# One plain gate/up pair fewer in every FFN, ScalarE's and VectorE's order in gate/up fixed, and the fourth product ahead of the third

## The chip, the cores and the metric

The kernel runs on one core of a Trainium2 chip. The metric is the device time of one execution in microseconds; the time before is the median of three runs. A change of less than about 0.2% is not told from none.

## What is computed

Two layers of a decoder trunk on 512 tokens of width 1024, in float32. Each layer has an FFN with half weight, a mixer (a gated linear recurrence beside a windowed attention) and a second FFN with half weight, each between two RMS norms. The change touches the gate/up part of the four FFNs:

```python
def swiglu(h, w_gate, w_up, w_down):
    return (jax.nn.silu(h @ w_gate) * (h @ w_up)) @ w_down

for l in range(DEPTH):                       # DEPTH = 2, D_MODEL = 1024, D_FF = 2816
    h = rms_norm(x, gn[0])
    x = x + 0.5 * rms_norm(swiglu(h, w_ffn1_gate[l], w_ffn1_up[l], w_ffn1_down[l]), gn[1])
    ...                                      # the mixer
    h = rms_norm(x, gn[4])
    x = x + 0.5 * rms_norm(swiglu(h, w_ffn2_gate[l], w_ffn2_up[l], w_ffn2_down[l]), gn[5])
```

## The kernel before

**Numbers in two halves.** Each float32 operand is split into a high half (`hi`, rounded to float32r by a cast on ScalarE) and a low half (`lo`, what the rounding left). A product is three matmuls, hi by hi, hi by lo, lo by hi (`mm3`); the low half of the weights is used by the third. The low half is made in one of two ways: VectorE subtracts `hi` from the source (L332 for weights, L402 for values), or ScalarE writes the negated source, rounded as `hi` is, into `lo` (L329) and GpSimd issues a DMA that adds the source to it (L330).

**Gate/up.** D_FF = 2816 gives 22 column tiles of 128, each a gate tile and an up tile, called a pair here. The first two pairs are computed together in `quad`. Then come plain pairs: for gate and for up eight matmul triples of 512 columns (`project`), and `gated` multiplies Silu(gate) by up. After `PLAIN` pairs (`FIRST` in the very first FFN) the rest of the 22 is done in `fast`: each pair is a 2 x 2 block product with seven products instead of eight (`sevenths`), each product being four matmul triples of 256 columns. A seven-product pair needs, beside the raw values, sums over quarters of x: `pre.sums()` makes them in four rounds, each some additions on VectorE (L459 to L466, L564) and two splits (casts L401, subtractions L402). In the first FFN a round also scales x (L535) and splits it.

**Weights.** `Stream` brings weights from HBM in order: a raw ring `w32` of W32 = 4 tiles loaded by SyncE, and rings `whi` and `wlo` of WS = 6 tiles. A plain pair uses two raw tiles as they are (kind `u`, VectorE subtracts; kind `v`, low half by DMA). A seven-product pair makes four pieces of its two raw tiles, in this order: **a**, the first tile (low half by DMA; products 1 and 2), **b**, two additions on VectorE (L312, L313; products 5 and 7), **c**, two more additions on b (L318, L319; products 6 and 4), **d**, half of the second tile (low half by DMA; product 3). `ahead` splits up to `most` = AHEAD = 3 items past the current one while fewer than WS are in flight; what it splits stands in the program at that place.

**After the products.** In `sevenths` ScalarE copies product 1 (L865), VectorE combines (L875, L877, L882, L883) into `m`, which has one buffer; ScalarE takes Silu on half of it (L895) and VectorE multiplies into z (L896).

**What sets the order.** TensorE's order is that of the program. The other engines' instructions are ordered by a scheduler when the kernel is built, except that those given to `pin` keep the program's order among themselves. In before only some are pinned: the additions of b and c, and the gating multiplication.

The seven products in before, in order: 1 and 2 (piece a), 5 and 7 (b), 6 (c), 3 (d), 4 (c again).

Of the kernel before, what the change touches and what calls it, by code (L numbers as in the profile page):

```python
# [7 lines left out]
F32 = mybir.dt.float32  # L8
F32R = mybir.dt.float32r
I32 = mybir.dt.int32  # L10
AF = mybir.ActivationFunctionType
# [34 lines left out]
def trunk(ctx: ExitStack, tc: tile.TileContext, xin, wall, gains, lbT, hgain, sinks, c_dist, c_mask, c_ident, out):  # L46
# [12 lines left out]
    def nm(s):  # L59
        seq[0] += 1  # L60
        return f"{s}_{seq[0]}"
# [94 lines left out]
    class Stream:  # L156
        def __init__(self):
            self.n, self.wall = 0, 0
            self.items = []
            self.raw, self.dma = {}, 0  # L160
            self.done, self.flight = 0, 0
            self.cur, self.c = 0, 0
            self.src = {}
            self.pinned = False
            self.most = AHEAD
            self.side, self.freed = {}, 0

        def plain(self, n, kind="u"):
# [86 lines left out]
        def quarter(self, it):  # L255
# [34 lines left out]
            if it.kind in ("p5", "p4"):  # L290
                self.raw.pop(it.u)
                self.freed += 1
                self.load(self.freed + W32)

        def split(self):
            it = self.items[self.done]
            if it.kind[0] == "p":
                return self.quarter(it)
            u, last = it.u, it.kind in "uvd"
            self.load(u + (1 if it.kind in "uv" else 2))  # L300
            it.hi = sb.tile([P, D], F32R, tag="whi", name=nm("whi"), bufs=WS)
            it.lo = sb.tile([P, D], F32R, tag="wlo", name=nm("wlo"), bufs=WS)
            w, h = self.raw[u], (slice(0, D // 2), slice(D // 2, D))
            cols = (slice(0, D),)
            if it.kind == "u" and u == 0:
                cols = h
            if it.kind in "bcd":
                v = self.raw[u + 1]
            if it.kind == "b":

                self.t13 = sb.tile([P, D], F32, tag="tt", name=nm("tt"), bufs=2)
                pin(nc.vector.tensor_tensor(self.t13[:, h[0]], w[:, h[0]], v[:, h[0]], op=ALU.add))  # L312
                pin(nc.vector.tensor_tensor(self.t13[:, h[1]], v[:, h[0]], v[:, h[1]], op=ALU.add))  # L313
                w = self.t13
            elif it.kind == "c":

                t = sb.tile([P, D], F32, tag="tt", name=nm("tt"), bufs=2)
                pin(nc.vector.tensor_tensor(t[:, h[0]], self.t13[:, h[0]], v[:, h[1]], op=ALU.add))  # L318
                pin(nc.vector.tensor_tensor(t[:, h[1]], t[:, h[0]], w[:, h[1]], op=ALU.add))  # L319
                w = t  # L320
            elif it.kind == "d":
                w = v
                cols = h[1:]
            for c in cols:
                i = nc.scalar.copy(it.hi[:, c], w[:, c])  # L325
                if u < 3 or self.pinned:
                    pin(i)
                if it.kind in "vad":
                    nc.scalar.mul(it.lo[:, c], w[:, c], -1.0)  # L329
                    nc.gpsimd.dma_start(it.lo[:, c].bitcast(F32), w[:, c], accum_op=ALU.add)  # L330
                else:
                    nc.vector.tensor_tensor(it.lo[:, c], w[:, c], it.hi[:, c].bitcast(F32), op=ALU.subtract)  # L332
# [64 lines left out]
    def split(src, scale=None, to=None):  # L397

        hi, lo = to or (big(F32R), big(F32R))
        if scale is None:  # L400
            nc.scalar.copy(hi, src)  # L401
            nc.vector.tensor_tensor(lo, src, hi.bitcast(F32), op=ALU.subtract)  # L402
# [448 lines left out]
    def sevenths(pre, between=lambda: None):  # L851

        def product(o, it, c, n):
            x = pre.operand(n)
            for k in range(4):
                wmm(o, ws.block(it, c + k), x[k], k == 0, k == 3)

        p1, p26, p57, p43 = acc()[:, :H2], acc(), acc(), aux()  # L860
        s, v = big()[:, :H2], big(F32, [P, 2, H2])
        m = sb.tile([P, 4, H2], F32, tag="m", name=nm("m"), bufs=1)
        w = ws.whole()
        product(p1, w, 0, 1)
        nc.scalar.copy(s, p1)  # L865
# [9 lines left out]
        nc.vector.tensor_tensor(m[:, 0:4:2, :], pairs[0], s.unsqueeze(1).to_broadcast([P, 2, H2]), op=ALU.add)  # L875

        nc.vector.tensor_tensor(v, pairs[1], m[:, 2:3, :].to_broadcast([P, 2, H2]), op=ALU.add)  # L877
        w = ws.whole()
        product(p43[:, H2:], w, 4, 3)
        product(p43[:, :H2], c, 4, 4)  # L880

        nc.vector.tensor_tensor(m[:, 3, :], p57[:, :H2], v[:, 1, :], op=ALU.add)  # L882
        nc.vector.tensor_tensor(m[:, 1:3, :], pairs[2], v[:, ::-1, :], op=ALU.add)  # L883
        return m

    def fast(pre, a, start):
        def early():
            if j == FT - 1:
                for i in range(EARLY):
                    a[i] = split(a[i])  # L890

        for j in range(start, FT):
            m = sevenths(pre, early)
            z = big(F32, [P, 2, H2])
            nc.scalar.activation(out=m[:, 0:2, :], in_=m[:, 0:2, :], func=AF.Silu)  # L895
            nc.vector.scalar_tensor_tensor(z, m[:, 0:2, :], -1.0, m[:, 2:4, :], op0=ALU.mult, op1=ALU.mult)  # L896
            a.append(z.rearrange("p i t -> p (i t)"))

    def ffn(l, n, pre, nxt, halves=True):
        a = []  # L900
# [24 lines left out]
        if first:  # L925
            gated(o[4], o[5])
            for j in range(3, FIRST):
                if j > 3:
                    order.until(lambda: pre.laid)
                    pre.sums()  # L930
                if j == 4:
                    pre.sums()
                gated(project(pre), project(pre))
            fast(pre, a, FIRST)
        else:
            for j in range(2, PLAIN):
                pre.sums()
                gated(project(pre), project(pre))
            fast(pre, a, PLAIN)
# [512 lines left out]
```

## Time and profile before

| | |
|---|---|
| median of three runs | 2100.99 us (2100.95 to 2102.06) |
| profiled execution | 2100.66 us |
| its span, first to last instruction | 2098.9 us |
| granted TensorE clock, mean | 0.999 |
| busy: PE, PEld, DVE, ACT, POOL | 100%, 89%, 74%, 53%, 7% |

Names in the profile: PE is the matmul stream of TensorE and PEld its weight load, DVE is VectorE, ACT ScalarE, POOL GpSimd, SP SyncE. L115 is the line in `mm` that issues matmuls, so matmuls are told apart by the tiles they write: a plain pair writes `acc` tiles with 512 columns, a seven-product pair three `acc` tiles and one `aux` tile with 256 columns. In a timeline row the first number is the start in microseconds from the span's start, the second the duration; brackets give idle time of the engine before it and what ended it. A DMA row ends with the size in KB and the time from issue to landing in microseconds.

### The profile page before, as it was taken

The page shows a single profiled execution, that of the slowest core. Times are in us where ns is not written, and L with a number is a line of the kernel's source. Part 1 is how long each engine was busy: PE and PEld are TensorE (multiplying, and loading weights), DVE is VectorE, ACT ScalarE, POOL GpSimd, SP SyncE. Part 2 cuts the span into 40 slices and gives each one's busy share as a digit, 9 for nine tenths or more (in the row PEclk, how much of TensorE's full clock was granted, in tenths as well). Part 3 has the DMA queues.
Part 4 walks back from the last instruction along what each step waited for, and adds up shares of the span by engine and source line. Part 5 has one row for each costly group of instructions (what it writes and reads, how often), then busy time and mean ns, then how long its engine had stood idle before and what let it go on. Part 6 is the DMA issues. An engine that isn't in the chain of part 4 may idle for free.

```text
span 2098.9 us, 35207 instructions
## 1 busy us (share of the span) xinstructions
PE 2090.3 (100%) x13549; PEld 1875.3 (89%) x13549; DVE 1550.5 (74%) x2705; ACT 1122.4 (53%) x1899; POOL 154.2 (7%) x188
## 2 busy tenths in 40 slices
PE   9999999999999999999999999999999999999998
PEld 8899988887888999998899998898778989999987
DVE  5877886766776777789587778767687758777884
ACT  6555564456454555556455556554653545555562
POOL 0011000000000011110001110000000000111000
PEclk9999999999999999999999999999999999999999
DMA  8577653312236357774447775632122563677651
GB/s 246 152 181 184 178 157 135 111 61 71 71 101 203 127 122 182 181 198 122 154 114 176 183 181 150 191 120 92 51 81 61 136 193 103 159 182 181 184 160 51
DMA packets 148071, 298.35 MB, mean 142 GB/s; under 512 B 16992, under 2 KB 74816, under 8 KB 147904
## 3 DMA queue, kind: packets, MB, share of 16 engines
q1 hardware_dynamic: 122416, 228.16, 33.2%
q0 software_dynamic: 25344, 67.91, 18.7%
q8 instruction: 106, 1.74, 0.3%
q14 instruction: 61, 0.50, 0.1%
q10 hardware_dynamic: 144, 0.05, 0.0%
HBM read 213.43 MB, written 14.73 MB: 109 GB/s over the span
## 4 chain that ended last, share of the span: by engine, by line
PE 88%; DMA 0%; DVE 0%; ACT 0%; SPq 0%; issue 0%; ACTq 0%
PE acc L115 64%; PE aux L115 22%; PE aux L125 1%; PE acc L125 1%; DMA wlo<-w 0%; DMA w<-wall 0%; SPq L241 0%; DVE s L402 0%; ACT whi L282 0%; DVE s L731 0%; ACT s L600 0%; DVE s L712 0%; DVE s L896 0%; DVE wlo L287 0%; ACT m L895 0%
## 5 line engine op out<-in xcount | busy, mean ns | idle before, releaser
L115 PE MATMUL acc<-s,whi 128*128 128x256 f32 (+1 forms) x4952 | 1059.3, 311 | 0.4 <-ACT whi L325 0.3
L115 PEld LDWEIGHTS acc<-s,whi 128*128 128x128 f32 x4952 | 808.0, 191 | 51.3 <-issue 3.2
L115 PE MATMUL acc<-s,wlo 128*128 128x256 f32 (+1 forms) x2476 | 766.6, 310 | 0.1
L115 PEld LDWEIGHTS acc<-s,wlo 128*128 128x128 f32 x2476 | 472.6, 191 | 25.0 <-DVE wlo L332 0.4
L325 ACT CAST whi<-w 128x1024 fp32r<-128x1024 f32 (+1 forms) x341 | 316.6, 948 | 237.6 <-PE acc L115 95.5
L115 PE MATMUL acc<-whi,s 128*128 128x512 f32 x1264 | 413.6, 393 | 0.1
L325 ACT CAST whi<-tt 128x1024 fp32r<-128x1024 f32 x154 | 161.4, 1048 | 326.5 <-DVE tt L319 184.2
L332 DVE TENSOR_TENSOR wlo<-w,whi 128x1024 fp32r<-128x1024 f32 (+1 forms) x181 | 218.3, 1215 | 151.4 <-ACT whi L325 149.6
L115 PEld LDWEIGHTS acc<-whi,s 128*128 128x128 f32 x1264 | 237.1, 188 | 54.7 <-ACT whi L325 1.6
L332 DVE TENSOR_TENSOR wlo<-tt,whi 128x1024 fp32r<-128x1024 f32 x154 | 188.1, 1221 | 98.8 <-ACT whi L325 98.7
L115 PE MATMUL acc<-wlo,s 128*128 128x512 f32 x632 | 246.4, 390 | 0.0
L115 PE MATMUL aux<-s,whi 128*128 128x256 f32 (+1 forms) x1248 | 230.4, 285 | 0.0
L330 POOL DMA_DIRECT2D wlo<-w x160 | 137.8, 863 | 1258.6 <-ACT wlo L329 704.9
L115 PE MATMUL aux<-whi,s 128*128 128x512 f32 x592 | 196.7, 390 | 0.0
L115 PEld LDWEIGHTS aux<-s,whi 128*128 128x128 f32 x1248 | 195.2, 192 | 1.1 <-issue 0.5
L115 PE MATMUL aux<-s,wlo 128*128 128x256 f32 (+1 forms) x624 | 177.5, 284 | 0.0
L115 PEld LDWEIGHTS acc<-wlo,s 128*128 128x128 f32 x632 | 118.7, 188 | 23.4
L115 PEld LDWEIGHTS aux<-whi,s 128*128 128x128 f32 x592 | 111.1, 188 | 22.8
L329 ACT ACTIVATE wlo<-w 128x1024 fp32r<-128x1024 f32 (+1 forms) x160 | 129.8, 844 | 0.0
L401 ACT CAST s<-s 128x512 fp32r<-128x512 f32 (+1 forms) x164 | 88.4, 580 | 71.5 <-DVE s L460 67.9
L115 PEld LDWEIGHTS aux<-s,wlo 128*128 128x128 f32 x624 | 119.8, 192 | 0.3
L115 PE MATMUL aux<-wlo,s 128*128 128x512 f32 x296 | 115.2, 389 | 0.0
(186 smaller groups left out, 2128.6 us busy)
## 6 DMA issues: line engine op xcount, KB each, us to landing
w<-wall SPq DMA_DIRECT2D x267, 512.0 KB, 3.7
wlo<-w POOLq DMA_DIRECT2D x83, 512.0 KB, 5.5
w<-wall SPq DMA_DIRECT2D x288, 128.0 KB, 3.3
wlo<-w POOLq DMA_DIRECT2D x77, 256.0 KB, 3.3
x_d<-s SPq DMA_DIRECT2D x48, 256.0 KB, 2.1
s<-x_d SPq DMA_DIRECT2D x48, 256.0 KB, 5.5
w<-wall SPq DMA_DIRECT2D x34, 256.0 KB, 3.0
s<-wall SPq DMA_DIRECT2D x64, 128.0 KB, 3.6
```

What stands on the lines that cost most here:

```text
L115: nc.tensor.matmul(o, lhsT, rhs, start=start, stop=stop)
L125: nc.tensor.transpose(o, src, ident)
L325: i = nc.scalar.copy(it.hi[:, c], w[:, c])
L329: nc.scalar.mul(it.lo[:, c], w[:, c], -1.0)
L330: nc.gpsimd.dma_start(it.lo[:, c].bitcast(F32), w[:, c], accum_op=ALU.add)
L332: nc.vector.tensor_tensor(it.lo[:, c], w[:, c], it.hi[:, c].bitcast(F32), op=ALU.subtract)
L401: nc.scalar.copy(hi, src)
```

## The change

It does five things. `PLAIN` goes from 4 to 3 and `FIRST` from 7 to 6, so each FFN has one plain pair fewer and one seven-product pair more; the four rounds of sums are issued within the pairs that are left. Inside `fast` (`ws.tight`) the casts, the multiplications by -1, the subtractions, the copy of product 1, the combinations, Silu and z are pinned to the program's order. The multiplication into z is held back (`ws.gate`) and issued behind the additions of the next b that is split, or before the next `m` is taken. Product 4 comes ahead of product 3, so that piece c is done before d is needed. And `most` is AHEAD + 1 in all but the last seven-product pair. The order of products 4 and 3 also changes in the mixer's `branches`, which use `sevenths` without the pinning.

```diff
-W32, WS, AHEAD, TAIL, PLAIN, FIRST, EARLY, LATE = 4, 6, 3, 4, 4, 7, 4, 8
+W32, WS, AHEAD, TAIL, PLAIN, FIRST, EARLY, LATE = 4, 6, 3, 4, 3, 6, 4, 8
...
+        def hold(self, i):
+            if self.tight:
+                pin(i)
+
+        def product(self):
+            if self.gate:
+                self.gate()
+                self.gate = None
...  (in Stream.split, kind b, behind the two additions)
+                self.product()
...
                 i = nc.scalar.copy(it.hi[:, c], w[:, c])
-                if u < 3 or self.pinned:
+                if u < 3 or self.pinned or self.tight:
                     pin(i)
                 if it.kind in "vad":
-                    nc.scalar.mul(it.lo[:, c], w[:, c], -1.0)
+                    self.hold(nc.scalar.mul(it.lo[:, c], w[:, c], -1.0))
                     nc.gpsimd.dma_start(it.lo[:, c].bitcast(F32), w[:, c], accum_op=ALU.add)
                 else:
-                    nc.vector.tensor_tensor(it.lo[:, c], w[:, c], it.hi[:, c].bitcast(F32), op=ALU.subtract)
+                    self.hold(nc.vector.tensor_tensor(it.lo[:, c], w[:, c], it.hi[:, c].bitcast(F32), op=ALU.subtract))
...  (in sevenths)
-        m = sb.tile([P, 4, H2], F32, tag="m", name=nm("m"), bufs=1)
...
-        nc.scalar.copy(s, p1)
+        ws.hold(nc.scalar.copy(s, p1))
...
         product(p26[:, H2:], c, 0, 6)
+        ws.product()
+        m = sb.tile([P, 4, H2], F32, tag="m", name=nm("m"), bufs=1)
...  (the four combinations are held likewise)
-        w = ws.whole()
-        product(p43[:, H2:], w, 4, 3)
         product(p43[:, :H2], c, 4, 4)
+        product(p43[:, H2:], ws.whole(), 4, 3)
...  (in fast)
+        ws.tight = True
         for j in range(start, FT):
+            ws.most = AHEAD + (j < FT - 1)
             m = sevenths(pre, early)
             z = big(F32, [P, 2, H2])
-            nc.scalar.activation(out=m[:, 0:2, :], in_=m[:, 0:2, :], func=AF.Silu)
-            nc.vector.scalar_tensor_tensor(z, m[:, 0:2, :], -1.0, m[:, 2:4, :], op0=ALU.mult, op1=ALU.mult)
+            ws.hold(nc.scalar.activation(out=m[:, 0:2, :], in_=m[:, 0:2, :], func=AF.Silu))
+
+            def gate(m=m, z=z):
+                ws.hold(nc.vector.scalar_tensor_tensor(z, m[:, 0:2, :], -1.0, m[:, 2:4, :], op0=ALU.mult, op1=ALU.mult))
+
+            ws.gate = gate
+            if j == FT - 1:
+                ws.product()
             a.append(z.rearrange("p i t -> p (i t)"))
+        ws.tight = False
...  (in ffn, first FFN)
                 if j > 3:
                     order.until(lambda: pre.laid)
                     pre.sums()
-                if j == 4:
                     pre.sums()
...  (other FFNs)
             for j in range(2, PLAIN):
+                pre.sums()
                 pre.sums()
```

Three places show what moved in the built programs. The numbers in the rows of before and after are different names for the same kind of tile; after's lines stand 11 to 20 further down.

First, VectorE in the first FFN, where piece b of the first seven-product pair stands (L312, L313, L332 in before). Before, behind the third round of sums (its last two subtractions, L402):

```order
L402 TENSOR_TENSOR s_734<-s_727,s_733 128x512
L402 TENSOR_TENSOR s_738<-s_728,s_737 128x512
L312 TENSOR_TENSOR tt_798<-w_92_503,w_104_567 128x512
L313 TENSOR_TENSOR tt_798<-w_104_567 128x512
L332 TENSOR_TENSOR wlo_797<-tt_798,whi_796 128x1024
L905 TENSOR_TENSOR s_803<-acc_741,s_395 128x512
L907 TENSOR_TENSOR s_804<-acc_771,s_395 128x512
```

After, behind the second round, ahead of the gating (L925, L927) of the plain pair that in before stood ahead of the third round:

```order
L413 TENSOR_TENSOR s_639<-s_632,s_638 128x512
L413 TENSOR_TENSOR s_643<-s_633,s_642 128x512
L322 TENSOR_TENSOR tt_703<-w_72_384,w_78_437 128x512
L323 TENSOR_TENSOR tt_703<-w_78_437 128x512
L343 TENSOR_TENSOR wlo_702<-tt_703,whi_701 128x1024
L925 TENSOR_TENSOR s_708<-acc_646,s_395 128x512
L927 TENSOR_TENSOR s_709<-acc_676,s_395 128x512
```

Piece b moved ahead of one gating step and of the third round. Between the third and the fourth round in after stands nothing, where before had piece b and one gating step; piece c follows the fourth round in both.

Second, ScalarE at the same entry: the casts of pieces c (`whi<-tt`), d and the next pair's a, with the multiplications for the low halves, and the Silu of the last plain pair. Before:

```order
L325 CAST whi_859<-tt_861 128x1024
L325 CAST whi_891<-w_104_567 128x512
L329 ACTIVATE wlo_892<-w_104_567 128x512
L325 CAST whi_916<-w_133_676 128x1024
L906 ACTIVATE s_900<-s_900 128x512
L329 ACTIVATE wlo_917<-w_133_676 128x1024
```

After:

```order
L336 CAST whi_789<-tt_791 128x1024
L336 CAST whi_821<-w_78_437 128x512
L340 ACTIVATE wlo_822<-w_78_437 128x512
L926 ACTIVATE s_830<-s_830 128x512
L336 CAST whi_842<-w_92_503 128x1024
L340 ACTIVATE wlo_843<-w_92_503 128x1024
```

The Silu, which waits for VectorE's gating step, moved ahead of the cast of the next pair's piece a.

Third, VectorE in a pair in the middle of gate/up, from the combinations to the next pair's. Before:

```order
L875 TENSOR_TENSOR m_8299<-acc_8294,s_8297 128x2x256
L877 TENSOR_TENSOR s_8298<-acc_8295,m_8299 128x512
L332 TENSOR_TENSOR wlo_8365<-tt_8366,whi_8364 128x1024
L882 TENSOR_TENSOR m_8299<-acc_8295,s_8298 128x256
L883 TENSOR_TENSOR m_8299<-aux_8296,s_8298 128x512
L896 SCALAR_TENSOR_TENSOR s_8417<-m_8299 128x512
L312 TENSOR_TENSOR tt_8462<-w_1484_8263,w_1485_8265 128x512
L313 TENSOR_TENSOR tt_8462<-w_1485_8265 128x512
L332 TENSOR_TENSOR wlo_8461<-tt_8462,whi_8460 128x1024
```

After:

```order
L887 TENSOR_TENSOR m_8379<-acc_8289,s_8292 128x2x256
L889 TENSOR_TENSOR s_8293<-acc_8290,m_8379 128x512
L893 TENSOR_TENSOR m_8379<-acc_8290,s_8293 128x256
L894 TENSOR_TENSOR m_8379<-aux_8291,s_8293 128x512
L322 TENSOR_TENSOR tt_8426<-w_1483_8239,w_1484_8241 128x512
L323 TENSOR_TENSOR tt_8426<-w_1484_8241 128x512
L911 SCALAR_TENSOR_TENSOR s_8413<-m_8379 128x512
L343 TENSOR_TENSOR wlo_8425<-tt_8426,whi_8424 128x1024
```

The multiplication into z (L896, now L911) moved behind the additions of b, and c's subtraction, which stood among the combinations, now stands ahead of them.

More of the change, by code (lines that the diff above doesn't have):

```diff
@@ L165, in __init__ @@
             self.most = AHEAD
+            self.tight, self.gate = False, None
             self.side, self.freed = {}, 0
@@ L872, in sevenths @@
         product(p26[:, H2:], c, 0, 6)
+        ws.product()
+        m = sb.tile([P, 4, H2], F32, tag="m", name=nm("m"), bufs=1)
         pairs = [p.rearrange("p (i t) -> p i t", i=2) for p in (p26, p57, p43)]
[L875 to L879 removed]
+        ws.hold(nc.vector.tensor_tensor(m[:, 0:4:2, :], pairs[0], s.unsqueeze(1).to_broadcast([P, 2, H2]), op=ALU.add))
+        ws.hold(nc.vector.tensor_tensor(v, pairs[1], m[:, 2:3, :].to_broadcast([P, 2, H2]), op=ALU.add))
         product(p43[:, :H2], c, 4, 4)
[L882 to L883 removed]
+        product(p43[:, H2:], ws.whole(), 4, 3)
+        ws.hold(nc.vector.tensor_tensor(m[:, 3, :], p57[:, :H2], v[:, 1, :], op=ALU.add))
+        ws.hold(nc.vector.tensor_tensor(m[:, 1:3, :], pairs[2], v[:, ::-1, :], op=ALU.add))
         return m
```

4 lines of the change are left out of this document (2 added, 2 removed).

## The prediction

> **What bounds the kernel now.** I read the page first, then the chain of waits over a stretch of gate/up, the busy time of single pairs, and then the timelines at the place where an FFN passes from its plain pairs to its seven-product pairs.
>
> ```profile
> span 2098.9 us, 35207 instructions
> PE 2090.3 (100%) x13549; PEld 1875.3 (89%) x13549; DVE 1550.5 (74%) x2705; ACT 1122.4 (53%) x1899; POOL 154.2 (7%) x188
> PE 88%; DMA 0%; DVE 0%; ACT 0%; SPq 0%; issue 0%; ACTq 0%
> ```
>
> TensorE is busy for the whole span and alone carries the chain that ended last. No other engine has more than rounding on it. Inside the seven-product pairs it is as dense as that:
>
> ```profile
> 761.06 2.88 PE aux L115 x24
> 763.94 7.20 PE acc L115 x60
> 771.14 2.88 PE aux L115 x24
> 784.10:794.18 10.08, 10.08 (x86) 10.08 (x86) 7.76 (x12) 5.70 (x9) 1.72 (x2) 1.00 0.77 184
> ```
>
> A pair is 60 matmuls in three acc tiles (five products, 1.44 us each) and 24 in one aux tile (two products): 7.20 + 2.88 = 10.08 us, with the next pair right behind. The last row is one such pair by engines: PE, PEld, DVE, ACT, POOL, clock. VectorE works 7.76 us of 10.08, ScalarE 5.70. So gate/up has no idle TensorE time to win back. The change can take away matmul time, and it can open waits.
>
> **What it takes away.** These are TensorE's rows in the first FFN: the start of the fifth plain pair, then the first seven-product pair with its third matmul, then the second seven-product pair.
>
> ```profile
> 57.01 0.71 PE L115 MATMUL acc<-s,whi 128*128 128x512 f32 x2
> 89.75 0.40 PE L115 MATMUL acc<-s,whi 128*128 128x256 f32 x2
> 89.98 0.28 PE L115 MATMUL acc<-s,wlo 128*128 128x256 f32 x1
> 99.82 0.40 PE L115 MATMUL acc<-s,whi 128*128 128x256 f32 x2
> ```
>
> From 57.01 to 89.75 stand three plain pairs, so one is 32.74 / 3 = 10.91 us. A seven-product pair is 10.08. One pair changed in each of four FFNs: 4 x (10.91 - 10.08) = **-3.3 us**. That is all the gain there is, and it is 0.16% of the time, less than the 0.2% that a measurement here can tell from no change.
>
> **What it moves.** Every FFN enters its seven-product pairs one plain pair, 10.91 us, earlier. What must be ready by then is VectorE's work (the sums over quarters of x, four rounds, and pieces b and c of the weights) and the GpSimd transfers that make the low halves of pieces a and d. So I walk the entry of the first FFN with the rows of before, in the order of after.
>
> ```profile
> 71.23 0.67 DVE L905 TENSOR_TENSOR s<-acc,s 128x512 f32<-128x512 f32 x1
> 77.05 0.68 DVE L312 TENSOR_TENSOR tt<-w,w 128x512 f32<-128x512 f32 x1
> 80.65 0.68 DVE L905 TENSOR_TENSOR s<-acc,s 128x512 f32<-128x512 f32 x1
> 81.25 0.68 DVE L907 TENSOR_TENSOR s<-acc,s 128x512 f32<-128x512 f32 x1
> 82.19 0.68 DVE L908 TENSOR_TENSOR s<-s,s 128x512 f32<-128x512 f32 x1
> 86.49 0.69 DVE L318 TENSOR_TENSOR tt<-tt,w 128x512 f32<-128x512 f32 x1
> 89.08 1.23 DVE L332 TENSOR_TENSOR wlo<-tt,whi 128x1024 fp32r<-128x1024 f32 x1 [1.17 <-ACT whi L325]
> 90.22 0.68 DVE L905 TENSOR_TENSOR s<-acc,s 128x512 f32<-128x512 f32 x1
> 88.00 1.05 ACT L325 CAST whi<-tt 128x1024 fp32r<-128x1024 f32 x1 [2.22 <-DVE tt L319]
> 88.95 0.62 ACT L325 CAST whi<-w 128x512 fp32r<-128x512 f32 x1
> 89.47 0.63 ACT L329 ACTIVATE wlo<-w 128x512 fp32r<-128x512 f32 x1
> 90.00 1.04 ACT L325 CAST whi<-w 128x1024 fp32r<-128x1024 f32 x1
> 91.00 0.63 ACT L906 ACTIVATE s<-s 128x512 f32<-128x512 f32 x1
> 91.53 1.04 ACT L329 ACTIVATE wlo<-w 128x1024 fp32r<-128x1024 f32 x1
> 92.87 0.86 POOL L330 DMA_DIRECT2D wlo<-w  x1 [1.62 <-ACT s L865]
> wlo<-w POOLq DMA_DIRECT2D x1, 512.0 KB, 6.1
> ```
>
> VectorE has hardly a gap here: gating and third sums 71.23 to 77.05 (5.82 us), piece b to 80.65 (3.60), gating (three starts 0.60 apart, 1.80 together) and fourth sums to 86.49 (5.84), then piece c, whose cast starts on ScalarE at 88.00, 1.51 later. In the order of after, b stands ahead of gating and third sums, and the fourth sums follow without gating between: 71.23 + 3.60 + 5.82 + (5.84 - 1.80) = 84.69, and c's cast at 86.20. VectorE gains 1.8 us by the shorter queue; TensorE wants everything 10.91 us earlier, with its first seven-product pair at 89.75 - 10.91 = 78.84.
>
> Piece c is wanted by the sixth product's third matmul, after four products: 78.84 + 5.76 + 0.23 = 84.83. Its cast starts at 86.20, its subtraction 1.08 later (89.08 - 88.00) and that ends 1.14 later, at 88.42: 3.6 us late. Piece d's cast and multiplication follow on ScalarE (87.15, 87.67), then in after the Silu of the last plain pair, now ahead of the next piece a. It waits for VectorE's first gating step behind c's subtraction: 88.42 + 0.68 = 89.10, Silu to 89.65 (0.53 as 91.00 to 91.53). Then a's cast and multiplication, 0.95 each, to 91.55. GpSimd starts its transfer 0.39 after that (92.87 against 91.53 + 0.95), at 91.95. It lands 5.2 us (the other rows below) to 6.1 us later: 97.15 to 98.05. TensorE wants it in the third matmul of the second pair, 78.84 + 10.07 + 0.23 = 89.14. So it is 8.0 to 8.9 us late; I take **+8.5**, nearer to the transfer of this very piece. The lateness of the earlier pieces is contained in it and not added. In the kernel before the same transfer landed at 92.87 + 6.1 = 98.97 for a need at 100.05, with only 1.1 us in hand.
>
> The other three FFNs have shorter sums. Rows of layer 0's second FFN, and three landings of 512 KB from GpSimd:
>
> ```profile
> 739.61 0.68 DVE L312 TENSOR_TENSOR tt<-w,w 128x512 f32<-128x512 f32 x1
> 743.16 0.68 DVE L911 TENSOR_TENSOR s<-acc,s 128x512 f32<-128x512 f32 x1
> 743.76 1.28 DVE L564 TENSOR_TENSOR s<-s,s 128x512 f32<-128x512 f32 x2
> 753.70 0.40 PE L115 MATMUL acc<-s,whi 128*128 128x256 f32 x2
> 753.86 0.86 POOL L330 DMA_DIRECT2D wlo<-w  x1 [1.04 <-PE acc L115]
> wlo<-w POOLq DMA_DIRECT2D x1, 512.0 KB, 5.0
> wlo<-w POOLq DMA_DIRECT2D x1, 512.0 KB, 5.2
> wlo<-w POOLq DMA_DIRECT2D x1, 512.0 KB, 4.5
> w<-wall SPq DMA_DIRECT2D x267, 512.0 KB, 3.7
> ```
>
> Before: a of the second pair lands at 753.86 + 5.0 = 758.9 for a need at 753.70 + 10.07 + 0.23 = 764.0, 5.1 us in hand. (The 5.2 is the same transfer at layer 1's second FFN; 4.5 is one with no load beside it. The last row is what a plain load of that size takes.) After: b (3.55 us, 739.61 to 743.16) and the gating step (0.60) leave the queue ahead of c, so the chain to this transfer is 4.15 earlier, and the need 10.91 earlier. 5.1 + 4.15 - 10.91 = -1.65. b's additions reappear ahead of the first sums, where two subtractions of plain weights fall away, which may save a few tenths: between 0.8 and 2.2 late, taken as **+1.5** for each of three, +4.5.
>
> In the steady pairs the new order costs nothing if VectorE's queue fits: 7.76 us of work and at most two exposed casts of 1.05 (as at 88.00), 9.9 in 10.08. TensorE covers that; b and c are made almost a pair ahead. Swapping products 4 and 3 leaves 84 matmuls and frees c 1.44 us sooner, which the same cover hides. At the end of gate/up the pinned order only brings the four early splits of the gated values forward. Nothing else is on the path.
>
> Sum: -3.3 + 8.5 + 4.5 = +9.7. The profiled execution took 2100.66 (its span 2098.9 and 1.8 around it), 0.33 under the median of the runs, 2100.99. So 2110.4 by the profiled execution, **2110.7** as a median.
>
> **Two rules weighed.** The 512 KB transfers from GpSimd take 4.5 to 6.1 us to land in this trace. The Trainium skill (DMA: Bandwidth & Descriptors, Anatomy of one DMA) fits a GpSimd-issued transfer as 2.0 us plus its bytes over 436 KB a microsecond, here an estimate of 3.2 us; by that the sum would be about +2.7, 2103.7. No row of such a transfer agrees, and the rows decide. (Rival 4 prices a quicker landing from rows.)
>
> ```profile
> 2090.00:2094.00 4.00, 1.05 (x7) 0.46 (x5) 3.04 (x6) 1.02 (x3) 0.00 (x0) 1.00 0.43 131
> 2094.00:2099.00 5.00, 0.86 (x4) 0.45 (x4) 0.62 (x1) 0.59 (x1) 0.00 (x0) 0.52 0.34 105
> ```
>
> After four microseconds in which TensorE worked 1.05, the granted clock (third number from the end) was 0.52. The last wait at the first FFN's entry would be 8.5 less the 3.6 to 4.1 spent on c and d, a gap of over 4 us. The Trainium skill (TensorE: Matmul & The Clock Gate, Why this matters for your kernels) says that an idle gap of more than about 3 us drops the clock to half, which speaks against this change and agrees with the second row; rival 1 prices it.
>
> **Rivals.** (1) *Half clock after the gap.* If the clock falls there and stays down about as long as the gap, 4.4 us, half of it is lost, 2.2 us: 2112.9. For it speak the two rows; against, that those four microseconds were about as long as this gap and the fall came only behind them. 0.15. (2) *Only the first FFN waits*, the other three being saved by a transfer without load beside it and sums that begin sooner: 2100.99 - 3.3 + 8.5 = 2106.2. 0.07. (3) *Not slower: the entries stay hidden.* Piece a needs nothing of VectorE; if its cast and transfer run well ahead of c's, the wait vanishes and 2100.99 - 3.3 = 2097.7 is left. This decides at one point: a's transfer in the first FFN must start by 89.14 - 5.2 = 83.9. Against it stands ScalarE's queue, where a's cast is behind c's and behind the Silu. 0.07. (4) *Quick landing.* If a's transfer landed like a plain load, in 3.7 us, the first FFN would be 91.95 + 3.7 - 89.14 = 6.5 late and the others 1.5 - 1.3 = 0.2: 2100.99 - 3.3 + 6.5 + 0.6 = 2104.8. 0.04. (5) *VectorE becomes the bound of the steady pairs.* If its fixed order needs 10.8 us instead of 9.9, 18 pairs lose 0.7 each over 10.08, 12.6, of which the lead of some 8 us hides most: 4.6 in each of four FFNs, with the entries 2129. 0.04. My forecast holds 0.63.
>
> **The numbers.** The forecast's own bounds are 8.0 + 3 x 0.8 - 3.3 = +7.1 (2108.1) and 8.9 + 3 x 2.2 - 3.3 = +12.2 (2113.2). With rivals 1 and 2 the range is 2106.0 to 2114.5. Slower by over 0.2% (above 2105.2): 0.63 + 0.15 + 0.07 + 0.04 = 0.89. Rivals 3 and 4 lie within 0.2%; for a gain beyond 3.3 us I see no source, but leave it 0.02 and take that from both: 0.88 slower, 0.10 same.
>
> **What would show it.** Right: in the first FFN the second seven-product pair starts near 97 instead of 88.9, TensorE's largest wait there is for wlo written by the GpSimd transfer, and the pairs after it are 10.08 apart. At the other entries a wait of 1 to 2 us at the same place. Wrong: entries without a gap, a pair period above 10.08, or waits for sums instead of weights.

## The result and the profile after

The changed kernel took 2113.89 us (median of 6 runs, 2112.99 to 2114.71), the kernel before beside it 2101.10 (2100.01 to 2102.06). The ratio is 1.0062, with a 95% interval of 1.0051 to 1.0073: 10.7 to 15.3 us slower. The forecast was 2110.7, +9.7.

The span and the busy time of the changed kernel, from its page:

```profile
span 2112.2 us, 35822 instructions
PE 2091.4 (99%) x13693; PEld 1882.7 (89%) x13693; DVE 1579.6 (75%) x2737; ACT 1146.2 (54%) x1917; POOL 159.8 (8%) x194
```

From the view of waits, TensorE's over the whole span (us in all, times, longest), those for weights:

```profile
PE acc L115 <- DMA wlo<-w: 8.8, 4, 5.0
PE acc L115 <- ACT whi L336: 1.6, 2, 1.1
PE acc L115 <- DVE wlo L343: 0.8, 1, 0.8
```

The span is 13.3 us longer (2112.2 against 2098.9). In the kernel before no wait for a weight was longer than 0.3. Now four waits for a low half that came by DMA stand there, one of 5.0, and some for piece c (L336, L343). These are the rows of the first FFN's entry in the timeline: TensorE, then what the wait of 4.96 goes back to.

```profile
79.04 0.40 PE L115 MATMUL acc<-s,whi 128*128 128x256 f32 x2
93.39 0.40 PE L115 MATMUL acc<-s,whi 128*128 128x256 f32 x2
98.75 0.58 PE L115 MATMUL acc<-s,wlo 128*128 128x256 f32 x1 [4.96 <-DMA wlo<-w]
111.05 0.40 PE L115 MATMUL acc<-s,whi 128*128 128x256 f32 x2
86.37 1.04 ACT L336 CAST whi<-tt 128x1024 fp32r<-128x1024 f32 x1 [2.22 <-PE acc L115]
87.45 1.23 DVE L343 TENSOR_TENSOR wlo<-tt,whi 128x1024 fp32r<-128x1024 f32 x1 [1.17 <-ACT whi L336]
89.37 0.63 ACT L926 ACTIVATE s<-s 128x512 f32<-128x512 f32 x1 [0.90 <-DVE s L925]
90.84 1.06 ACT L340 ACTIVATE wlo<-w 128x1024 fp32r<-128x1024 f32 x1
92.19 0.86 POOL L341 DMA_DIRECT2D wlo<-w  x1 [2.57 <-DVE tt L323]
```

And the transfer that this last row issues, in the view of DMA (us from issue to landing):

```profile
wlo<-w POOLq DMA_DIRECT2D x1, 512.0 KB, 6.5
```

From the start of the first seven-product pair (79.04) to that of the third (111.05) pass 32.01 us, where two pairs need 20.16: 11.85 lost at this entry. Some 4 of them come in the first pair, for sums, piece c and piece d (93.39 - 79.04 is 14.35 where 10.08 are needed); then the third matmul of the second pair waits 4.96 for the low half of a. The 2.4 that are left are seen in the windows (the number third from the end is the granted clock):

```profile
95.00:99.00 4.00, 0.25 (x1) 0.25 (x2) 2.80 (x4) 3.26 (x5) 0.86 (x1) 0.79 0.71 151
99.00:103.00 4.00, 4.00 (x20) 4.00 (x21) 3.38 (x7) 2.62 (x4) 0.86 (x1) 0.50 0.94 227
103.00:107.00 4.00, 4.00 (x31) 4.00 (x31) 2.77 (x4) 1.25 (x3) 0.00 (x0) 0.85 0.86 230
```

Behind the wait TensorE worked without a gap, but at half clock until about 104: 20 matmul rows in four microseconds; the next four, of which a quarter is still at half clock, have 31. By the matmuls' starts in the trace 23 steps were 0.09 longer than the usual 0.12: 2.1 us, and the first step behind the wait 0.3 longer. The other three entries, in the order of the program:

```profile
763.72 0.40 PE L115 MATMUL acc<-s,whi 128*128 128x256 f32 x2
765.51 0.39 PE L115 MATMUL acc<-s,wlo 128*128 128x256 f32 x1 [1.40 <-DMA wlo<-w]
1107.95 0.39 PE L115 MATMUL aux<-s,wlo 128*128 128x256 f32 x1 [0.36 <-DMA wlo<-w]
1109.25 0.40 PE L115 MATMUL acc<-s,whi 128*128 128x256 f32 x2
1110.66 0.38 PE L115 MATMUL acc<-s,wlo 128*128 128x256 f32 x1 [1.01 <-DMA wlo<-w]
1803.48 0.40 PE L115 MATMUL acc<-s,whi 128*128 128x256 f32 x2
1805.29 0.39 PE L115 MATMUL acc<-s,wlo 128*128 128x256 f32 x1 [1.41 <-DMA wlo<-w]
```

The third matmul of a pair normally starts 0.23 after the first; here 1.79, 1.41 and 1.81. So 1.6 are lost at the second entry, 1.2 and about 0.5 for piece d at the third, 1.6 at the fourth: 4.9. By the starts of the pairs (the distance from one pair's first matmul to the next pair's, less 10.08) it is 1.6, 1.9 and 1.7, or 5.2. The account closes to half a microsecond: 11.85 + 4.9 to 5.2 - 3.3 = 13.4 to 13.8, against 13.3 between the spans.

### The profile page after: what moved, and what is told of

Read it like the earlier page. It is cut to its first block, busy times and chain, and to the rows that moved or that the text cites. A ratio compares the mean times of both kernels' runs of the same rounds, so it can differ in the third digit from the quotient of the medians.

```text
span 2112.2 us, 35822 instructions
## 1 busy us (share of the span) xinstructions
PE 2091.4 (99%) x13693; PEld 1882.7 (89%) x13693; DVE 1579.6 (75%) x2737; ACT 1146.2 (54%) x1917; POOL 159.8 (8%) x194
## 4 chain that ended last, share of the span: by engine, by line
PE 94%; issue 4%; DMA 2%; ACT 0%; DVE 0%; POOL 0%; SPq 0%; POOLq 0%
PE acc L115 68%; PE aux L115 24%; PE aux L125 1%; DMA wlo<-w 1%; PE acc L125 1%; DMA w<-wall 0%; DMA s<-xin 0%; DMA g_sb<-gains 0%; ACT s L512 0%; ACT whi L336 0%; POOL wlo L341 0%; SPq L1320 0%; DVE s L742 0%; DVE s L513 0%; ACT s L442 0%
## 5 line engine op out<-in xcount | busy, mean ns | idle before, releaser
L336 ACT CAST whi<-w 128x1024 fp32r<-128x1024 f32 (+1 forms) x341 | 320.1, 943 | 255.7 <-PE aux L115 96.3
L343 DVE TENSOR_TENSOR wlo<-w,whi 128x1024 fp32r<-128x1024 f32 (+1 forms) x175 | 210.8, 1216 | 148.3 <-ACT whi L336 145.7
L336 ACT CAST whi<-tt 128x1024 fp32r<-128x1024 f32 x162 | 169.8, 1048 | 251.3 <-DVE tt L330 190.9
L343 DVE TENSOR_TENSOR wlo<-tt,whi 128x1024 fp32r<-128x1024 f32 x162 | 198.6, 1226 | 142.6 <-ACT whi L336 142.6
L115 PE MATMUL aux<-s,whi 128*128 128x256 f32 (+1 forms) x1312 | 242.2, 285 | 0.0
L341 POOL DMA_DIRECT2D wlo<-w x166 | 143.3, 864 | 1251.2 <-DVE wlo L343 501.8
L115 PEld LDWEIGHTS aux<-s,whi 128*128 128x128 f32 x1312 | 205.2, 192 | 1.1 <-issue 0.5
L115 PE MATMUL aux<-s,wlo 128*128 128x256 f32 (+1 forms) x656 | 186.7, 285 | 0.6 <-DMA wlo<-w 0.6
L340 ACT ACTIVATE wlo<-w 128x1024 fp32r<-128x1024 f32 (+1 forms) x166 | 140.3, 845 | 0.0
L115 PEld LDWEIGHTS aux<-s,wlo 128*128 128x128 f32 x656 | 125.9, 192 | 1.3 <-DMA wlo<-w 1.0
```

What stands on the lines that cost most here:

```text
L115: nc.tensor.matmul(o, lhsT, rhs, start=start, stop=stop)
L340: self.hold(nc.scalar.mul(it.lo[:, c], w[:, c], -1.0))
L343: self.hold(nc.vector.tensor_tensor(it.lo[:, c], w[:, c], it.hi[:, c].bitcast(F32), op=ALU.subtract))
```

## The experiments

Theory A says that the loss is at the four entries, by the late transfer of piece a and the half clock behind it, and that the new order itself is free. The rivals give other places. All ratios are against the kernel before on the same chip.

| kernel | median us | ratio (95% interval) |
|---|---|---|
| only the first FFN put back | 2105.61 | 1.0022 (1.0013 to 1.0031) |
| only the other FFNs put back | 2110.74 | 1.0047 (1.0034 to 1.0060) |
| new order, all pairs put back | 2101.20 | 1.0003 (0.9994 to 1.0013) |
| one pair fewer, nothing pinned | 2152.61 | 1.0246 (1.0232 to 1.0260) |
| the same, ScalarE's order fixed | 2161.18 | 1.0293 (1.0278 to 1.0307) |
| changed, piece a in halves | 2108.67 | 1.0039 (1.0026 to 1.0051) |
| first FFN put back, a in halves | 2104.72 | 1.0019 (1.0010 to 1.0028) |
| first FFN put back, c early | 2100.04 | 0.9997 (0.9988 to 1.0006) |
| the same, a earlier too | 2100.26 | 0.9996 (0.9987 to 1.0004) |
| changed, long wait filled | 2113.91, again 2114.03 | 1.0063 (1.0050 to 1.0075), 1.0062 (1.0049 to 1.0075) |
| changed, again | 2113.53 | 1.0058 (1.0044 to 1.0071) |

**Only the first FFN put back.**

```diff
-W32, WS, AHEAD, TAIL, PLAIN, FIRST, EARLY, LATE = 4, 6, 3, 4, 3, 6, 4, 8
+W32, WS, AHEAD, TAIL, PLAIN, FIRST, EARLY, LATE = 4, 6, 3, 4, 3, 7, 4, 8
                 if j > 3:
                     order.until(lambda: pre.laid)
                     pre.sums()
+                if j == 4:
                     pre.sums()
```

> The changed kernel with the first FFN's entry put back (seven plain pairs there, its sums in the rounds of before); the other three FFNs keep one plain pair fewer, and the new order stays. Theory A (the loss lies at the entries: in the first FFN 9.4 us of waits and 2.1 us of half clock, 1.7 us at each other entry, and each pair changed gives 0.83): 2101.1 - 3 x 0.83 + 3 x 1.7 = 2103.7. Rival B (the fixed order of ScalarE and VectorE costs time in the steady pairs of all four FFNs, some 3 us each): about 2110. Rival C (the other entries are hidden, all of the loss is the first FFN's): 2098.6.

2105.61, +4.6 by the ratio (2.7 to 6.5). Theory A's 2103.7, which is +2.6, lies just under that interval; rivals B (+8.9) and C (-2.5) lie further outside. What theory A missed is in the view of waits: four waits for a's low half, 5.5 us together, the longest 2.1 (at the third entry), and one of them in the first FFN, where the new order alone costs 0.9 (below).

**Only the other FFNs put back.** `PLAIN` is 4 again and their plain pairs make one round of sums each; `FIRST` stays 6.

> The changed kernel with the other three FFNs put back to four plain pairs (one round of sums in each plain pair there, as before); the first FFN keeps six. Theory A: 2101.1 - 0.83 + 11.5 = 2111.8. Rival B (the order costs about 3 us in every FFN): about 2113. Rival C (all of the loss is the first FFN's): 2113.9 + 3 x 0.83 = 2116.4, since undoing the others would then only lose their gain.

2110.74, +9.9 (7.1 to 12.6), against theory A's +10.7. The view of waits has one wait for a's low half, of 4.1, in the first FFN, and none at the other entries. This ratio excludes rival C. B's 2113 lies inside the interval, near its upper edge; B falls by the run above and by the next one.

**The new order alone.** Both counts put back, and the rounds of sums as before.

> The changed kernel with both counts of plain pairs put back; what is left of the change is the pinned order, a piece more split ahead, and the fourth product ahead of the third. Theory A: no change, 2100.6 to 2101.6. Rival B (the order costs some 3 us in each FFN): 2110 or more. A third possibility, that the order gains by itself, would show as under 2100.

2101.20, ratio 1.0003, no difference that can be seen: theory A. The one new wait in its profile that is longer than 0.3 is 0.7 for a's low half at the first FFN's second seven-product pair; by the starts of the pairs 0.9 is lost there.

**One pair fewer, nothing pinned.** The kernel before with this alone:

```diff
-W32, WS, AHEAD, TAIL, PLAIN, FIRST, EARLY, LATE = 4, 6, 3, 4, 4, 7, 4, 8
+W32, WS, AHEAD, TAIL, PLAIN, FIRST, EARLY, LATE = 4, 6, 3, 4, 3, 6, 4, 8
...
-                if j == 4:
                     pre.sums()
...
             for j in range(2, PLAIN):
                 pre.sums()
+                pre.sums()
```

> The kernel before with one plain pair fewer in every FFN (and its rounds of sums moved so that all four stand ahead of the seven-product pairs), without the pinned order, with the third product ahead of the fourth. Theory A (TensorE wants everything 10.9 us earlier, whatever the order): 2111 to 2118, with the same wait for the low half of piece a in the first FFN. Rival D (the pinned order itself makes that wait, by putting a's cast behind c's and the Silu): 2098 to 2104.

2152.61: both were far off. Here the loss isn't at the entries alone. TensorE's waits for a's low half over the whole span:

```profile
PE acc L115 <- DMA wlo<-w: 27.1, 23, 2.4
```

That is 23 waits, spread over the seven-product pairs of all four FFNs. By the starts of the pairs, the first two pairs of each FFN lose 13.5 together here and 17.0 in the changed kernel, so the early entry costs time under either order. But theory A's "same wait" isn't there: in the first FFN a's transfer starts at 91.12 instead of 92.19, the half clock ends ahead of its landing (96.9), and the entry loses 7.8 instead of 11.9. In part, then, rival D is right.

The rest, some 37, is lost in the middle of gate/up, nearly all of it in every third pair. Two rows of the kernel before, ScalarE's Silu in two pairs that lie thirteen apart, show a part of the reason:

```profile
785.32 0.61 ACT L895 ACTIVATE m<-m 128x512 f32<-128x512 f32 x1
917.91 0.62 ACT L895 ACTIVATE m<-m 128x512 f32<-128x512 f32 x1
```

(917.91 - 785.32) / 13 = 10.20 us: in the kernel before ScalarE's round of one pair takes 0.12 more than TensorE's 10.08. It works off a lead, and TensorE never sees it, since the FFN ends before the lead does. With the entry 10.9 us earlier there is less of a lead. But 0.12 in each of 73 pairs is 9 us at most. The order is another one too: what isn't pinned, the scheduler orders anew in each kernel. VectorE's second addition of c (L319) and its first combination (L875), first in the kernel before, then here:

```profile
862.23 0.69 DVE L319 TENSOR_TENSOR tt<-tt,w 128x512 f32<-128x512 f32 x1
862.84 0.68 DVE L875 TENSOR_TENSOR m<-acc,s 128x512 f32<-128x512 f32 x1
```

```profile
858.90 0.69 DVE L875 TENSOR_TENSOR m<-acc,s 128x512 f32<-128x512 f32 x1 [2.26 <-PE acc L115]
859.51 0.68 DVE L319 TENSOR_TENSOR tt<-tt,w 128x512 f32<-128x512 f32 x1
```

In the kernel before the addition stands ahead in 61 of 69 pairs; here the combination does, in 65 of 73. In the row shown the combination waits 2.26 for TensorE's products; c's addition stands behind it, a's cast behind c's, and TensorE waits for a. VectorE is idle ahead of this combination 39 times, 64 us together, against 9 times and 7 us in the kernel before. So this run is not the old order with one pair fewer; what the shorter lead and what the other order costs was not separated.

ScalarE's Silu in the changed kernel, after the late entry and later in that FFN:

```profile
778.38 0.63 ACT L908 ACTIVATE m<-m 128x512 f32<-128x512 f32 x1 [0.79 <-DVE m L894]
826.89 0.63 ACT L908 ACTIVATE m<-m 128x512 f32<-128x512 f32 x1 [0.35 <-DVE m L894]
836.92 0.63 ACT L908 ACTIVATE m<-m 128x512 f32<-128x512 f32 x1 [0.30 <-DVE m L894]
847.00 0.63 ACT L908 ACTIVATE m<-m 128x512 f32<-128x512 f32 x1 [0.29 <-DVE m L894]
```

Five pairs from 778.38 to 826.89 are 9.70 each; from 836.92 on it is 10.08, at TensorE's pace. The new order's round is shorter than TensorE's, so a late start is caught up in a few pairs. Against the order that the scheduler builds for one pair fewer, the new order is worth 2152.6 - 2113.9, some 39 us. What it would be worth against the order of the kernel before, held by pins, no run shows.

**The same with ScalarE's order fixed.** In the run before, one pair of three had a's cast behind the Silu. So that was undone, one piece more was split ahead, and VectorE was left to the scheduler:

```diff
-                if u < 3 or self.pinned:
+                if u < 3 or self.pinned or self.tight:
...
-                    nc.scalar.mul(it.lo[:, c], w[:, c], -1.0)
+                    self.hold(nc.scalar.mul(it.lo[:, c], w[:, c], -1.0))
...
+            ws.most = AHEAD + (j < FT - 1)
             m = sevenths(pre, early)
...
-            nc.scalar.activation(out=m[:, 0:2, :], in_=m[:, 0:2, :], func=AF.Silu)
+            ws.hold(nc.scalar.activation(out=m[:, 0:2, :], in_=m[:, 0:2, :], func=AF.Silu))
```

> The kernel with one plain pair fewer and no pinned order (2152.6), plus one piece more split ahead and ScalarE's order alone fixed in the seven-product pairs: the casts and multiplications of the weights ahead of the pair's Silu. VectorE's order and the order of the products stay as before. In the profile without pins TensorE waited 23 times, 27.1 us together, for the low half of piece a, and in each group of three pairs there is one in which a's cast stood behind the Silu. Theory J (the Silu ahead of a's cast makes these waits): they go, and the time is that of the changed kernel, 2112 to 2115. Rival K (VectorE's order, with the combining steps ahead of the subtractions of the weights, makes them): 2135 to 2152.

2161.18, slower still. Theory J has fallen, and K is nearer, though it did not foresee a loss beyond 2152.6. The rows show a round that closes on itself. (The line numbers differ between the kernels; the Silu of a seven-product pair is L895, L902 or L908, the multiplication into z behind it L896, L903 or L911.) First this kernel's VectorE from one multiplication into z to the next and the piece b behind it, with the Silu between; then the same place in the changed kernel.

```profile
865.24 0.69 DVE L903 SCALAR_TENSOR_TENSOR s<-m 128x512 f32<-128x512 f32 x1 [2.25 <-ACT m L902]
875.12 0.61 ACT L902 ACTIVATE m<-m 128x512 f32<-128x512 f32 x1
875.77 0.69 DVE L903 SCALAR_TENSOR_TENSOR s<-m 128x512 f32<-128x512 f32 x1 [2.24 <-ACT m L902]
876.38 0.68 DVE L317 TENSOR_TENSOR tt<-w,w 128x512 f32<-128x512 f32 x1
```

```profile
866.98 0.68 DVE L322 TENSOR_TENSOR tt<-w,w 128x512 f32<-128x512 f32 x1
868.18 0.69 DVE L911 SCALAR_TENSOR_TENSOR s<-m 128x512 f32<-128x512 f32 x1
```

With the Silu behind a's cast, VectorE waits 2.24 for it in its multiplication into z, and piece b's additions (L317) are queued behind that. They begin the next chain: b, c, d, a, Silu. One round is 875.77 - 865.24 = 10.53, 0.45 over TensorE's, in most pairs. In the changed kernel b's additions (the first of them L322) stand ahead of the multiplication (L911), and there it waits for nothing. VectorE's waits at this step over the whole span, of the kernel before, of this one, and of the changed one:

```profile
DVE s L896 <- ACT m L895: 75.8, 65, 1.3
```

```profile
DVE s L903 <- ACT m L902: 148.8, 69, 2.2
```

```profile
DVE s L911 <- ACT m L908: 6.2, 4, 1.9
```

But the kernel before has the same round: a's cast ahead of the Silu, the multiplication ahead of b, a wait of 1.25, and 10.20 in all. What differs is again what the scheduler did with VectorE: here two combinations stand ahead of c's additions and a third between them, in 61 pairs, and the round is 0.33 longer. By these rows, of the 0.45 over TensorE's pace 0.33 goes with the place of the combinations, and at most 0.12 is left for the multiplication's. The changed kernel fixes both, and with them the order of the products; none of the three was tried by itself. What the runs do show is that ScalarE's order without VectorE's gains nothing.

**Piece a in two halves.** In the changed kernel:

```diff
-            if it.kind == "u" and u == 0:
+            if it.kind == "a" or it.kind == "u" and u == 0:
                 cols = h
```

> The changed kernel with every piece a cast, negated and transferred in two halves of 256 KB, the first of which product 1 needs and the second product 2, 1.44 us later. Theory A (the last link at every entry is the landing of a's 512 KB, 5.3 to 6.9 us; the 256 KB of piece d landed in 3.3): in the first FFN the wait falls from 9.4 to about 6 and the half clock goes, at the other entries 1.7 becomes 0 to 0.5: 2100.6 - 3.3 + 6 + 0 to 1.5 = 2103.3 to 2104.8. Rival F (two halves share the same engines and land no sooner than the whole): 2112 to 2114.

2108.67, +8.2 (5.5 to 10.7): 5 us better than the changed kernel, between theory A and rival F. In the first FFN the wait of 4.96 became these two, for the first and the second half, whose landings follow:

```profile
96.23 0.39 PE L115 MATMUL acc<-s,wlo 128*128 128x256 f32 x1 [1.14 <-DMA wlo<-w]
98.12 0.39 PE L115 MATMUL acc<-s,wlo 128*128 128x256 f32 x1 [0.19 <-DMA wlo<-w]
```

```profile
wlo<-w POOLq DMA_DIRECT2D x1, 256.0 KB, 4.6
wlo<-w POOLq DMA_DIRECT2D x1, 256.0 KB, 5.4
```

So a's transfer is the last link there, as theory A has it. But the halves took 4.6 and 5.4 to land, not the 3.3 that piece d's 256 KB took in the kernel before, and the second came at 98.1, hardly ahead of the whole (98.7); what helped is that the first came 2.5 sooner and the second is needed 1.44 later. The half clock didn't go: it fell in the first pair instead. At the other entries 1.7 less was lost in this profile (3.5 against 5.2). The next run, with the first FFN put back, doesn't bear that out, and there rival F holds:

> The kernel with seven plain pairs in the first FFN and three in the others, with every piece a transferred in two halves. Theory A: the three waits of 1.7 (5.5 in the profile) go or nearly so: 2105.2 less 4 to 5.5 = 2099.7 to 2101.2. Rival F (halves land no sooner): 2104 to 2106. Below 2100.6 it would beat both kernels by a little.

2104.72, the same as without halves (1.0019 against 1.0022, intervals overlapping). In layer 0's second FFN the two halves landed in 4.2 and 6.0 us from issue, with piece d's transfer in flight ahead of them. At the third entry this profile has a wait of 2.73.

**Piece c early.** From the kernel with the first FFN put back:

```diff
             for j in range(2, PLAIN):
                 pre.sums()
+                o = project(pre), project(pre)
                 pre.sums()
-                gated(project(pre), project(pre))
+                gated(*o)
```

> The changed kernel with seven plain pairs in the first FFN again, and in the other three FFNs the fourth round of sums moved behind piece c on VectorE (its additions stand ahead of that round's). Theory A (the chain to a's transfer there runs through VectorE's queue ahead of c, so c's additions some 1.5 to 4 us earlier bring the transfer about 1.5 us earlier): the waits of 1.7 fall to 0 to 0.5, time 2105.2 (1.0022 x 2100.6) less 3.6 to 5 = 2100.2 to 2101.6. Rival G (the sums themselves or the Silu of the last plain pair set the transfer's start): 2104 to 2106.

2100.04, ratio 0.9997 (0.9988 to 1.0006), against 1.0022 without it. The entry of layer 0's second FFN, GpSimd's issue and the third matmul; first as it was with the first FFN put back, then with c early:

```profile
749.93 0.86 POOL L341 DMA_DIRECT2D wlo<-w  x1 [1.03 <-DVE tt L323]
755.14 0.38 PE L115 MATMUL acc<-s,wlo 128*128 128x256 f32 x1 [1.29 <-DMA wlo<-w]
```

```profile
748.40 0.86 POOL L341 DMA_DIRECT2D wlo<-w  x1 [3.44 <-DVE tt L323]
753.93 0.39 PE L115 MATMUL acc<-s,wlo 128*128 128x256 f32 x1 [0.16 <-DMA wlo<-w]
```

The transfer starts 1.53 earlier and the wait falls by 1.13. So at these entries the chain through VectorE's queue ahead of c sets the transfer's start, as the prediction's step has it.

**The two together, and a earlier.** In the other FFNs `ws.most = AHEAD + 1` already ahead of the last plain pair, which puts a's cast ahead of the fourth sums' casts and the Silu; in the first FFN a goes in halves.

> The kernel with seven plain pairs in the first FFN and three in the others, the fourth round of sums behind piece c (as in the run before with c early), and two things more: in the other FFNs piece a of the second seven-product pair is split before that round's casts and the last Silu on ScalarE, and in the first FFN piece a goes in two halves. Theory A: the waits left in the other FFNs (0.4, 0.9 and 0.1 in the profile of c early) go because a's transfer starts 1.7 us sooner, and the 1.1 of the first FFN goes as it did with halves: 2100.55 - 2.5 = 2098.0, or 2098.0 to 2098.8. Rival H (a's casts ahead of the sums make the fourth round late for the fifth product, about 1 us in each of three FFNs): 2100 to 2101.

2100.26, 0.9996 (0.9987 to 1.0004). Theory A's 2098.0 to 2098.8 was missed; the number is rival H's, but its place only in part. At three entries no wait stood out in the profile; in the third FFN 0.5 was lost in the first seven-product pair, where the fourth round of sums came late as rival H has it, and 1.2 for a's low half in the fifth, which neither foresaw. The three pairs changed are worth 2.5 us at most, and 1.7 of it went there. This is the lowest ratio of all, but it can't be told from no change, so no version was found that beats the kernel before.

**The long wait filled.** To see what the half clock costs, 34 matmuls whose result is overwritten were put into the wait of the first FFN:

```diff
+                if fill and n == 1 and k == 0:
+                    b = ws.block(it, c)
+                    mm(o, b[2], x[0][0], True, False)
+                    mm(o, b[2], x[0][1], False, False)
+                    for _ in range(fill):
+                        mm(p43[:, :H2], b[2], x[0][0], True, True)
+                    mm(o, b[3], x[0][0], False, False)
```

> The changed kernel with 34 matmuls of 256 columns more (34 x 0.12 = 4.1 us), whose result is overwritten, put into TensorE's longest wait: in the first FFN's second seven-product pair, after the second matmul, ahead of the third that waits 5.1 us for the low half of piece a. They end before that transfer lands. Theory A (the clock fell to 0.50 from 99 to 104 us because TensorE stood idle, which cost 22 matmul steps of 0.09): the clock stays at 1.00 there and the time falls by 2.1 to about 2111.3, though work was added. Rival E (the slow steps behind the wait have another cause, such as the operands that arrive): the steps stay, and the time stays at 2113.4 (1.0062 x 2100.6).

> The changed kernel itself again, beside the next one on the same chip: 1.0062 of before, 2113.6.

> The kernel with 34 matmuls put into the long wait again. In its first profile the first FFN was 2.3 us shorter than in the changed kernel and the other entries 2.5 longer, with one wait of 2.3 and a half clock behind it. Theory A (that wait came from a transfer that happened to land late, and filling the long wait is worth 2 us): now 2 us below the changed kernel, 2111.5. Rival I (the whole stays equal whatever is filled): 2113.6.

2113.91 and 2114.03, against 2113.89 and 2113.53: nothing gained. Theory A's 2111.3 and 2111.5 lie at the edge of the intervals and below all ten runs. In the first profile the steps behind the wait did run at full clock, and the first FFN's entry lost 9.5 where the two profiles without filling lose 11.9 and 11.1. But the half clock came earlier, behind the 1.1 and 0.8 us that TensorE waits for piece c (as in the second profile of the changed kernel), and once more at the third entry, behind a wait of 2.1: 3.9 were lost there instead of 1.9. In the second profile the transfer took 8.3 us to land, so that 2.7 us of waiting were left behind the filling, the clock fell there (0.85 in the window from 99 to 103, 0.72 in the next), and the third entry lost 3.9 again. Why that entry lost more in both is not known.

So the half clock's share is seen in the profile of the changed kernel, over 2 us, but not shown to be worth that in the time. Whether this wait can be filled for a gain stays open.

## Why the prediction was right, point by point

**The sign and the place: right, the size 3 short.** Each FFN pays at its entry, for the low half of piece a of the second seven-product pair, and each pair changed gives less than it costs. Putting one or the other FFNs back shows both parts of the sum. The measured 2113.89 lies above the forecast's own upper bound of 2113.2. It is inside the range only because that was widened for rival 1.

**The chain in the first FFN: right step by step, 0.9 short.** TensorE's first seven-product pair started at 79.04 (78.84 foretold), c's cast at 86.37 (86.20), the Silu at 89.37 (89.10), the transfer at 92.19 (91.95). Its landing took 6.5, where I had taken 5.2 to 6.1. With 92.19 + 6.5 = 98.7 for a need at 79.04 + 10.30 = 89.34 it was 9.4 late instead of 8.5. (The three gating starts that I called 0.60 apart are 0.60 and 0.94 apart, with a subtraction between; they take 1.80 all the same.) One sign of it I had named wrongly: the second pair did not start near 97. Its first two matmuls don't need the low half; it started at 93.39 and its third matmul at 98.75.

**The clock: the term I left out.** Rival 1, which had 0.15, was a part of what happened: 23 steps at half clock in the first FFN's second pair. It said 2112.9, nearer to 2113.89 than my own 2110.7. The step that failed is the weighing of the two rows at the end of the kernel before: I held it against the rival that the fall came only behind those four microseconds. Here it came at 97.3, 1.4 us ahead of the gap's end, and lasted to 104.2, where the matmuls are. The Trainium skill (TensorE: Matmul & The Clock Gate, Why this matters for your kernels) says about 3 us of idling; the wait of 4.96 with 0.50 behind it agrees with that, while a wait of 2.35 with half clock behind it (below) is under its figure. That removing the fall gives its 2 us back is not shown.

**The other entries: right.** +1.5 each foretold, 1.6, 1.7 and 1.6 measured, at the places named; of the 1.7, some 0.5 is for piece d, which the sum did not have. In the run with c early the chain that I added up there was the one that counted.

**The new order free in the steady pairs: right, but for less than the whole reason.** I had 9.9 us for a round of VectorE; by the distance of the Silus it was 9.70, and alone the order cost nothing that the time shows. I did not see that the old order's round is 10.20. The prediction compared the changed kernel with before as if before's steady pairs had been safe; with nothing pinned, one pair fewer cost 52 us, in an order that the scheduler built anew.

**The DMA rule: the rows were right to decide.** The Trainium skill (DMA: Bandwidth & Descriptors, Anatomy of one DMA) gave an estimate of 3.2 us for such a transfer; measured were 6.5, 6.5, 6.7 and 8.3 for the same one in four profiles.

## What to carry to other kernels

Take a loop's period on every engine and not only its busy time: the distance between two of its instructions, many rounds apart, tells whether an engine that nobody waits for is living off a lead, and how long that lasts. Before a stage is entered earlier, find the last transfer that its first rounds need and the chain that starts it; the cover is that transfer's lead, and what is worth 0.83 us a pair must not cost more than that at the door. Where a scheduler sets an order, taking one part of a change back does not bring the old order back: compare the built orders before the times. And of an order that is fixed on two engines, neither half is to be judged alone.

## What the runs showed of the hardware that I had not expected

A short idle time is enough for the half clock. In the kernel with one pair fewer and nothing pinned, a wait, and the windows around it:

```profile
884.50 0.58 PE L115 MATMUL acc<-s,wlo 128*128 128x256 f32 x1 [2.35 <-DMA wlo<-w]
```

```profile
880.79:884.20 3.41, 1.35 (x12) 1.15 (x10) 3.27 (x6) 2.58 (x4) 0.19 (x1) 1.00 0.88 213
884.20:887.61 3.41, 3.11 (x14) 3.12 (x15) 1.77 (x4) 2.30 (x4) 1.53 (x2) 0.50 0.67 127
```

After 2.35 us of waiting the clock is at half for 3.41 us. Two waits of 1.1 and 0.8 within 3 us were followed by it in some profiles and not in others. These windows hold the same two waits, in the second profile of the changed kernel and then in its first:

```profile
85.37:88.78 3.41, 1.58 (x12) 1.17 (x10) 2.21 (x4) 2.10 (x3) 0.00 (x0) 1.00 0.37 108
88.78:92.19 3.41, 3.36 (x15) 3.36 (x16) 3.09 (x5) 2.60 (x4) 0.86 (x1) 0.50 0.56 123
```

```profile
87.10:90.51 3.41, 2.28 (x17) 2.08 (x18) 2.90 (x4) 2.51 (x5) 0.86 (x1) 1.00 0.57 172
90.51:93.93 3.42, 3.05 (x24) 2.64 (x22) 2.25 (x4) 2.71 (x4) 0.86 (x1) 1.00 0.59 104
```

So a gap's length alone does not tell whether it comes. Within a profile the starts of the half clock lie whole steps of 3.41 us apart. With all fourteen profiles cut into such steps, TensorE was busy for at most 1.6 us in every step that ended with a fall; of the steps at full clock without a fall behind them one had 1.5 and all others 1.8 or more. Where the steps lie differs from run to run, so the same wait can be cut in two by them, or not.
